# Ten of sixteen MLP blocks form their second product with seven block multiplications

## The chip, the cores and the metric

The kernel runs on one core of a Trainium2 chip. The metric is the device time of one execution in microseconds, as the median of several runs. TensorE multiplies matrices: a weight tile of 128 by 128 is loaded (PEld in the profile), then a moving operand of up to 512 columns streams past it (PE), and the product lands in one of eight PSUM banks. VectorE (DVE) and ScalarE (ACT) work on 128 partitions by some number of elements; SyncE (SP) issues all loads. Each engine runs its own instructions in order and waits on semaphores for the others.

## What is computed

The reference is two layers of a diffusion backbone on T = 1152 tokens (1024 latent, 128 context) of width 1024. Each layer has a token mixer (a Fourier mixer in layer 0, a gated recurrence called HGRN2 in layer 1), and then an MLP with a squared ReLU and a gate:

```
h = rmsnorm(x, norm_mlp[i]) * (1.0 + sc_f) + sh_f
x = x + gt_f * (jnp.square(jax.nn.relu(h @ mlp_w1[i])) @ mlp_w2[i])
```

`mlp_w1` is 1024 by 4096 and `mlp_w2` is 4096 by 1024. The six shift, scale and gate vectors of a layer come from a conditioning matrix `ada_w`.

## The kernel before, in words

Everything is float32. To keep that precision, each operand is split into a high part (`h`, rounded to the format that TensorE reads fast) and a low part (`l`, the rest). `split` does it with a ScalarE copy and a VectorE subtraction, and `mm3` makes three matmuls for each product: high by high, high by low, low by high.

The activations lie transposed, channels on partitions and tokens along the free axis, in three chunks of `CH` = 384 tokens. The MLP of a layer goes through `NBLK` = 8 blocks of four hidden tiles (`FB` = 4, 512 hidden channels). In a block the first product (`up`) takes four hidden tiles by three chunks, eight matmul triples each: 288 matmuls of 384 columns into banks of tag `z`. ScalarE makes ReLU and square, `split` makes the tiles `a0`, `a1`, `a2`. The second product (`out`) takes eight output tiles `d` by three chunks, four triples each: again 288 matmuls of 384 columns, into banks of tag `o`, and VectorE adds each result, times the gate, to the residual `x` in place (`residual`, L594). The weights of the first product come by `unit` (a load of 512 KB into `raw`, then `split`), those of the second by `w2` (256 KB into `raw2`).

Between these, VectorE makes the conditioning vectors (`ada_dve`, L181: two passes of 1024 elements for each of eight loads of a part). Layer 1 needs six such parts, one in each of the blocks 0 to 5 of layer 0, as the code is written. The pool `w` holds the w1 tiles and outlives the MLP; the pool `mlp0` or `mlp1` holds the rest of a block's tiles. A scheduler orders each engine's instructions by priority and readiness, so an instruction may stand well ahead of its place in the code, as far as its buffers allow. A pool that is opened where another was released gets its memory, and its tiles wait for the last use of what lay there.

Of the kernel before, what the change touches and what calls it, by code (L numbers as in the profile page):

```python
# [19 lines left out]
P = 128  # L20
D = 1024
KT = D // P
LS = 1024
LP = 128
T = LS + LP
CH = 384
NC = T // CH
GRID_W = 64
ROWS = LS // GRID_W
NF = 4 * D // P  # L30
FB = 4
NBLK = NF // FB
# [4 lines left out]
PASSES = ((0, 0), (0, 1), (1, 0))  # L37


def spans(c):  # L40

    a, b = c * CH, (c + 1) * CH
    out = []
# [7 lines left out]
def run_all(gen):  # L51
    for _ in gen:
        pass


class Net:
# [132 lines left out]
    def fnet(self):  # L189
# [281 lines left out]
        for d in range(KT):  # L471
# [24 lines left out]
            for xy, a, b, start, step, sc, op in (  # L496
# [40 lines left out]
    def rstd(self, chunks):  # L537

        nc = self.nc
        n = CH // P  # L540
        ps = self.t(self.ps, [P, 512], F32, "m", 2)
# [5 lines left out]
        N = n * len(chunks)  # L547
        r = self.t(self.tp, [P, n * NC], F32, "nrs", 2)[:, 0:N]
        nc.vector.tensor_scalar(out=r, in0=ps[:, 0:N], scalar1=1.0 / D, scalar2=EPS, op0=ALU.mult, op1=ALU.add)
# [45 lines left out]
                                                in1=xs, op0=ALU.mult, op1=ALU.add)  # L595


    def mlp(self, layer, before_chunk, before_block, after_chunk):
        nc, io = self.nc, self.io
        wp = self.pool(f"mlp{layer}")  # L600
        gt = self.mod.get((layer, 5))
# [56 lines left out]
        wp.release()  # L658


    def hgrn(self, xd, after_chunk):
# [312 lines left out]
    def run(self, stop=None):  # L974
        nc, io, tc = self.nc, self.io, self.tc
        self.setup()
        self.fnet()
        self.h = [None] * NC
        self.wp = self.pool("w")
        hp = self.hp = self.pool("hT")  # L980
        rbs = self.rms([0], "o") + self.rms([1, 2], "o")

        ap = self.pool("ada", side="right")

        def ada(blk):
# [3 lines left out]
            if blk < 6:  # L989
                run_all(self.ada_dve(1, blk, ap, ap, 2))  # L990
                if blk == 1:
                    self.make_A(1, 1, 1)
                if blk == 4:
                    self.make_A(1, 4, 3)
            if blk == NBLK - 1:
                ap.release()
                self.cond.release()

        self.mlp(0, lambda c: self.norm_h(c, rbs[c], self.A[0, 4], self.mod[0, 3]), ada, lambda c: self.norm_h(c, *self.rms([c], "m"), self.A[1, 1], self.mod[1, 0]))
# [43 lines left out]
        self.mlp(1, lambda c: None, lambda b: None, final)  # L1043
        dp.release()
        self.ps.release()
        hp.release()
        self.wp.release()
        self.tp.release()
        self.xp.release()
        self.cp.release()  # L1050
# [142 lines left out]
```

## Time and profile before

| | |
|---|---|
| median of 3 runs | 2661.19 us (2660.1 to 2661.51) |
| the profiled execution | 2665.3 us, of which the span in the profile 2663.5 us |
| TensorE busy | 2598.4 us, 98% |
| weight loads busy | 2505.6 us, 94% |
| VectorE busy | 1363.4 us, 51% |
| ScalarE busy | 882.0 us, 33% |
| mean granted TensorE clock | 0.989 |

The profiled execution is 4.1 us above the median of the runs; differences are worked out against it and taken off the median. Busy times of TensorE overlap, since matmuls are pipelined: a matmul's row lasts longer than the distance to the next one's start.

### The profile page before, as it was taken

Reading aid. Unit: us, or ns where it says so; the run is one execution under the profiler, and the core shown is the slowest. Engines: PE = TensorE matmul, PEld = TensorE weight load, DVE = VectorE, ACT = ScalarE, POOL = GpSimd, SP = SyncE. Lnnn points to the kernel's source line nnn. Section 1 sums busy time; section 2 is a strip of 40 time slices with the busy share of each in tenths; the row PEclk is TensorE's granted clock in tenths of the full one; section 3 lists DMA queues with packets and bytes.
Section 4 is the critical chain, followed back from the end, with each engine's and each line's share of the span. In section 5 each row is a group of like instructions: output and inputs, shape, how many; then the busy total and the mean of one; then the engine's idle time right before and its main releaser. Section 6 shows DMA issues by size and latency. Waiting matters only on the chain.

```text
span 2663.5 us, 45518 instructions
## 1 busy us (share of the span) xinstructions
PE 2598.4 (98%) x19446; PEld 2505.6 (94%) x19446; DVE 1363.4 (51%) x2437; ACT 882.0 (33%) x1757; POOL 35.8 (1%) x44
## 2 busy tenths in 40 slices
PE   6999999999999999999999999999999999999999
PEld 3788999999999999999989999899999999999998
DVE  7678998323323338465464664757323323323335
ACT  5435132132132244333432343424331231231232
POOL 0000000000000000000000000000000000000000
PEclk8899999999999999999999999999999999999999
DMA  7543565111111212111011011140111111111111
GB/s 258 185 164 102 172 188 149 47 44 38 47 44 39 58 36 88 33 37 37 29 36 40 31 29 35 37 136 17 56 40 40 48 40 40 48 40 40 48 32 72
DMA packets 65666, 180.00 MB, mean 68 GB/s; under 512 B 8204, under 2 KB 14860, under 8 KB 65464
## 3 DMA queue, kind: packets, MB, share of 16 engines
q1 hardware_dynamic: 65464, 177.09, 21.1%
q8 instruction: 153, 2.51, 0.4%
q14 instruction: 49, 0.40, 0.0%
HBM read 166.57 MB, written 10.49 MB: 66 GB/s over the span
## 4 chain that ended last, share of the span: by engine, by line
PE 87%; DVE 6%; DMA 3%; ACT 2%; issue 2%; POOL 1%; SPq 0%; DVEq 0%; POOLq 0%; ACTq 0%
PE z L91 45%; PE o L91 30%; PE z L729 4%; DMA adaw<-in_ada 2%; DVE junk L181 1%; DVE QK L822 1%; PE m L846 1%; PE o L770 1%; PE o L781 1%; PE m L839 1%; DVE hl L580 1%; PE o L159 0%; PE o L881 0%; ACT sT L785 0%; DVE tmp L577 0%
## 5 line engine op out<-in xcount | busy, mean ns | idle before, releaser
L91 PE MATMUL z<-hh,wh 128*128 128x384 f32 x2496 | 841.4, 338 | 3.9 <-issue 2.0
L91 PE MATMUL z<-hl,wh 128*128 128x384 f32 x2496 | 840.6, 337 | 0.0
L91 PE MATMUL z<-hh,wl 128*128 128x384 f32 x2496 | 838.4, 337 | 0.0
L91 PEld LDWEIGHTS z<-hh,wh 128*128 128x128 f32 x2496 | 468.7, 188 | 10.5 <-issue 3.0
L91 PEld LDWEIGHTS z<-hl,wh 128*128 128x128 f32 x2496 | 469.0, 188 | 3.9 <-DVE hl L580 1.4
L91 PEld LDWEIGHTS z<-hh,wl 128*128 128x128 f32 x2496 | 469.0, 188 | 1.0 <-DVE wl L82 0.2
L594 DVE SCALAR_TENSOR_TENSOR x<-o,mod,x 128x384 f32<-128x384 f32 (+2 forms) x512 | 253.1, 515 | 351.3 <-PE o L91 350.7
L82 DVE TENSOR_TENSOR wl<-raw,wh 128x1024 fp32r<-128x1024 f32 x113 | 138.2, 1223 | 294.4 <-ACT wh L81 294.4
L632 ACT CAST w<-raw 128x512 fp32r<-128x512 f32 x128 | 79.6, 622 | 617.1 <-PE o L91 600.7
L91 PE MATMUL o<-a1h,w 128*128 128x384 f32 x1024 | 280.4, 335 | 0.5 <-DVE x L594 0.5
L91 PE MATMUL o<-a0h,w 128*128 128x384 f32 x1024 | 279.8, 335 | 0.0
L91 PE MATMUL o<-a2h,w 128*128 128x384 f32 x1024 | 278.9, 334 | 0.0
L81 ACT CAST wh<-raw 128x1024 fp32r<-128x1024 f32 x113 | 118.6, 1051 | 271.5 <-PE z L91 229.5
L91 PEld LDWEIGHTS o<-a1h,w 128*128 128x128 f32 x1024 | 186.8, 188 | 1.3 <-DVE x L594 0.8
L91 PEld LDWEIGHTS o<-a0h,w 128*128 128x128 f32 x1024 | 187.4, 189 | 0.5 <-ACT a0h L81 0.2
L609 ACT ACTIVATE s<-z 128x384 f32<-128x384 f32 x192 | 93.6, 489 | 283.0 <-PE z L91 280.8
L91 PEld LDWEIGHTS o<-a2h,w 128*128 128x128 f32 x1024 | 186.6, 188 | 0.6 <-PE o L91 0.3
L91 PE MATMUL o<-a2l,w 128*128 128x384 f32 x512 | 171.9, 336 | 3.6 <-DVE a2l L82 3.6
L822 DVE TENSOR_TENSOR QK<-QK,F 128x1152 f32<-128x1152 f32 x112 | 164.7, 1504 | 17.3 <-ACT nacc L805 13.1
L91 PE MATMUL o<-a0l,w 128*128 128x384 f32 x512 | 171.8, 336 | 0.1
L91 PE MATMUL o<-a1l,w 128*128 128x384 f32 x512 | 171.2, 334 | 0.1
L181 DVE SCALAR_TENSOR_TENSOR junk<-adaw,s_rows 128x1024 bf16<-128x1024 f32 x112 | 136.7, 1220 | 16.7 <-DMA adaw<-in_ada 15.3
(256 smaller groups left out, 3038.0 us busy)
## 6 DMA issues: line engine op xcount, KB each, us to landing
adaw<-in_ada SPq DMA_DIRECT2D x96, 512.0 KB, 4.0
raw<-in_w SPq DMA_DIRECT2D x64, 512.0 KB, 3.6
raw<-in_w SPq DMA_DIRECT2D x128, 256.0 KB, 2.6
raw<-in_win SPq DMA_DIRECT2D x32, 512.0 KB, 3.5
x<-in_xT SPq DMA_DIRECT2D x8, 576.0 KB, 5.5
xd<-x SPq DMA_DIRECT2D x8, 576.0 KB, 2.9
raw<-in_who SPq DMA_DIRECT2D x9, 512.0 KB, 3.6
x<-xd SPq DMA_DIRECT2D x8, 576.0 KB, 5.8
```

Of the source, the lines that this page charges most:

```text
L81: nc.scalar.copy(out=hi, in_=src)
L82: nc.vector.tensor_sub(out=lo, in0=src, in1=hi.bitcast(F32))
L91: self.nc.tensor.matmul(out=out, lhsT=w[a], rhs=h[b], start=first and i == 0, stop=last and i == n - 1)
L181: nc.vector.scalar_tensor_tensor(out=jk, in0=w, scalar=1.0, in1=self.sb[:, b, :], op0=ALU.mult, op1=ALU.mult, accum_out=m[:, j, b:b + 1])
L580: ins = nc.vector.scalar_tensor_tensor(out=lo[:, d, l], in0=t[:, l], scalar=sh[:, d, q:q + 1], in1=hi[:, d, l].bitcast(F32), op0=ALU.add, ...
L594: self.nc.vector.scalar_tensor_tensor(out=xs, in0=ps[:, a - c * CH:b - c * CH], scalar=gt[:, d, q:q + 1], in1=xs, op0=ALU.mult, op1=ALU.add)
L609: nc.scalar.activation(out=s, in_=z, func=AF.Relu)
L632: nc.scalar.copy(out=w[:, 0], in_=raw)
L729: nc.tensor.matmul(out=half, lhsT=hs[c][a][:, KT // 2 * hf + k, o:o + P], rhs=ws[hf][b][:, k, :], start=hf == 0 and k == 0 and m == 0, sto ...
L770: nc.tensor.matmul(out=ps[32 * b:32 * b + 32, c, :], lhsT=lhs(c, b), rhs=rhs(c, b), start=True, stop=True)
L781: nc.tensor.matmul(out=ps[b * W:(b + 1) * W, i, :], lhsT=lhs(cs[0] + i, b), rhs=rhs(cs[0] + i, b ^ 1), start=True, stop=True)
L822: nc.vector.tensor_tensor(out=kv, in0=kv, in1=fv, op=ALU.mult)
```

## The change

In the blocks 3 to 6 of layer 0 and 1 to 6 of layer 1 the second product is done by the new function `mlp_seven`. It divides a block's product into 2 by 2 pieces three ways: the hidden tiles into even and odd (j), the outputs into the tiles d and d + 4 (l), and each half n of the tokens into two quarters (i) of `TQ` = 288. Sums and differences of the four activation pieces and of the four weight pieces are formed first (seven of each), then seven products (p = 0 to 6) replace eight, and they gather in three kinds of bank: `z` takes products 0, 2, 4 and 6, `o` product 1, `m` products 3 and 5. A bank that gathers is read out after each of its products and then added to further: each reading goes into another piece of `x`.

So a block's second product is 4 output pairs d by 7 products by 2 halves n by 2 hidden tiles by 3 passes = 336 matmuls of 288 columns, for 288 of 384 before. The first product keeps its matmuls; its weights come in two halves. ScalarE and VectorE have new work (`put`, the weight sums, 56 read-outs of 288 for 24 of 384). For the first pair, d = 0, the fourteen steps go half by half (all p for n = 0 first). The six conditioning parts of layer 1 are written into blocks 0 to 2 (one, three, two), since the memory of their pool is wanted from block 3 on. The pools `mlp` and `w` are released where the seven-product blocks begin and opened anew where they end; the pool `hT` is now opened ahead of `w`.

```
-    def mlp(self, layer, before_chunk, before_block, after_chunk):
+    def mlp(self, layer, before_chunk, before_block, after_chunk, seven):
...
         for blk in range(NBLK):
+            if blk == seven.start:
+                wp.release()
+                self.wp.release()
+                st = self.pool(f"seven{layer}")
+            if blk in seven:
+                self.mlp_seven(st, layer, blk)
+                before_block(blk)
+                continue
+            if blk == seven.stop:
+                st.release()
+                self.wp = self.pool("w")
+                wp = self.pool(f"mlp{layer}_")
...
+    def mlp_seven(self, st, layer, blk):
...
+            def put(p, n, src):
+
+                hi, lo = ah[k, n][:, p], al[k, n][:, p]
+                nc.scalar.copy(out=hi, in_=src)
+                nc.vector.tensor_sub(out=lo, in0=src, in1=hi.bitcast(F32))
...
+                for h in range(2):
+                    raw = self.t(st, [P, KT // 2, P], F32, "raw", 2)
+                    nc.sync.dma_start(out=raw, in_=io["w1"][layer, blk * FB + 2 * k + j][:, KT // 2 * h:KT // 2 * (h + 1)])
+                    w.append(self.split(st, raw, [P, KT // 2, P], "w", 3))
...
+                        nc.scalar.activation(out=q, in_=q, func=AF.Square)
+                        if j == 0 and i == 0:
+                            put(0, n, q)
+                        elif j == 0:
+                            s3 = self.tmp(TQ)
+                            nc.vector.tensor_sub(out=s3, in0=A[n, 0, 0], in1=q)
+                            put(4, n, s3)
+                        elif i == 0:
+                            put(1, n, q)
+                        else:
+                            put(6, n, q)
+                            a, b, s1 = A[n, 0, 0], A[n, 0, 1], A[n, 1, 0]
+                            nc.vector.tensor_add(out=s1, in0=s1, in1=q)
+                            nc.vector.tensor_sub(out=a, in0=s1, in1=a)
+                            put(2, n, a)
+                            put(3, n, s1)
+                            nc.vector.tensor_sub(out=b, in0=b, in1=a)
+                            put(5, n, b)
...
+            tt = self.t(st, [P, 3, FB // 2, P], F32, "tt", 1)
+            nc.vector.tensor_sub(out=tt[:, 0], in0=B[0, 1], in1=B[0, 0])
+            nc.vector.tensor_sub(out=tt[:, 1], in0=B[1, 1], in1=tt[:, 0])
+            nc.vector.tensor_sub(out=tt[:, 2], in0=B[1, 0], in1=tt[:, 1])
+            wa = self.split(st, raw[0], [P, FB // 2, 2, P], "wa", 1)
+            wb = self.split(st, tt[:, 0:2], [P, 2, FB // 2, P], "wb", 1)
+            nc.vector.tensor_sub(out=B[0, 1], in0=B[1, 1], in1=B[0, 1])
+            wc = self.split(st, raw[1], [P, FB // 2, 2, P], "wc", 1)
+            wd = self.split(st, tt[:, 2], [P, FB // 2, P], "wd", 1)
...
+            plan = (("z", 0, 0), ("o", 0, 0), ("z", 0, 1), ("m", 1, 1), ("z", 1, 1), ("m", 0, 1), ("z", 1, 0))
...
+            steps = [(p, n) for p in range(7) for n in range(2)]
+            if d == 0:
+                steps.sort(key=lambda s: s[1])
...
+                for k in range(FB // 2):
+                    for m, (x, y) in enumerate(PASSES):
+                        nc.tensor.matmul(out=ps, lhsT=W[p][k][x], rhs=(ah, al)[y][k, n][:, p, :],
...
+                        xs = self.x[d + KT // 2 * l][:, a:b]
+                        nc.vector.scalar_tensor_tensor(out=xs, in0=ps[:, a - t0:b - t0],
+                                                       scalar=gt[:, d + KT // 2 * l, q:q + 1], in1=xs,
+                                                       op0=ALU.mult, op1=ALU.add)
...
+        hp = self.hp = self.pool("hT")
         self.wp = self.pool("w")
-        hp = self.hp = self.pool("hT")
...
+            for part in ((0,), (1, 2, 3), (4, 5))[blk] if blk < 3 else ():
+                run_all(self.ada_dve(1, part, ap, ap, 2))
```

Three places of the order of instructions. The first is VectorE where the second product of a block of layer 1 begins. Before, the low parts of the last activation tiles (`a2l`) and the residuals of the first output tile alternate, with one waiting for each:

```order
L82 TENSOR_TENSOR a2l_23318<-s_23314,a2h_23317 128x384 [waits Activation_49]
L82 TENSOR_TENSOR a0l_23356<-s_23352,a0h_23355 128x384 [waits Activation_49]
L82 TENSOR_TENSOR a1l_23388<-s_23384,a1h_23387 128x384 [waits Activation_49]
L82 TENSOR_TENSOR wl_23912<-raw_23909,wh_23911 128x1024 [waits DVE_49,DMAHW6_49,PE_49,Activation_49]
L594 SCALAR_TENSOR_TENSOR x_2447_17257<-o_23428,mod_5_6993,x_2447_17257 128x384 [waits PE_49]
L82 TENSOR_TENSOR a2l_23420<-s_23416,a2h_23419 128x384 [waits Activation_49]
L594 SCALAR_TENSOR_TENSOR x_2447_17257<-o_23442,mod_5_6993,x_2447_17257 128x384 [waits PE_49]
```

In the changed kernel (a block in the middle of layer 1; L779 reads out a bank, L691 is `put`'s subtraction, L730 to L734 are sums) the same place reads:

```order
L83 TENSOR_TENSOR wl_23091<-raw_23088,wh_23090 128x512 [waits DMAHW7_49,PE_49,Activation_49]
L779 SCALAR_TENSOR_TENSOR x_2551_18141<-z_22471,mod_5_4613,x_2551_18141 128x288 [waits PE_49]
L730 TENSOR_TENSOR nacc_22209<-nacc_22209,tmp_22432 128x288 [waits Activation_49]
L691 TENSOR_TENSOR al_22208<-tmp_22401,ah_22207 128x288 [waits Activation_49]
L691 TENSOR_TENSOR al_22208<-tmp_22432,ah_22207 128x288 [waits Activation_49]
L731 TENSOR_TENSOR nacc_22209<-nacc_22209 128x288 [waits DVE_49]
L691 TENSOR_TENSOR al_22208<-nacc_22209,ah_22207 128x288 [waits Activation_49]
L734 TENSOR_TENSOR tmp_22401<-tmp_22401,nacc_22209 128x288 [waits DVE_49]
L691 TENSOR_TENSOR al_22208<-nacc_22209,ah_22207 128x288 [waits Activation_49]
L779 SCALAR_TENSOR_TENSOR x_2551_18141<-o_22479,mod_5_4613,x_2551_18141 128x288 [waits PE_49]
L691 TENSOR_TENSOR al_22208<-tmp_22401,ah_22207 128x288 [waits Activation_49]
L779 SCALAR_TENSOR_TENSOR x_2565_18285<-z_22471,mod_5_4613,x_2565_18285 128x288 [waits PE_49]
```

Between the first two readings of bank `z_22471` now stand ten instructions, eight of them for the second half's activations. TensorE has its third product for this bank, `z_22471<-ah_21964,wch_22463 [waits DVE_49]`, 43 matmuls behind the first of the second product.

The second place is SyncE ahead of the last block of layer 1 (the name in_w stands for both weights; L588 is the w1 load, L630 the w2 load). Before, the w1 loads of the last block stand ahead of the last four w2 loads of the block before it:

```order
L630 DMA raw_3257_23567<-in_w 128x512 [waits DMAHW4_49,DMAHW2_49,DVE_49]
L588 DMA raw_23807<-in_w 128x1024 [waits DVE_49]
L588 DMA raw_23909<-in_w 128x1024 [waits DVE_49]
L588 DMA raw_24011<-in_w 128x1024 [waits DMAHW5_49,DVE_49]
L588 DMA raw_24113<-in_w 128x1024 [waits DMAHW6_49,DVE_49]
L630 DMA raw_3262_23615<-in_w 128x512 [waits DMAHW3_49,DVE_49]
```

Now (L741 is the w2 load of `mlp_seven`, L589 the w1 load of the last block):

```order
L741 DMA raw_3525_25872<-in_w 128x512 [waits DMAHW5_49,DVE_49]
L741 DMA raw_3526_25874<-in_w 128x512 [waits DMAHW6_49,DVE_49]
L589 DMA raw_26011<-in_w 128x1024 [waits PE_49]
L589 DMA raw_26113<-in_w 128x1024 [waits PE_49]
L643 DMA raw_3603_26423<-in_w 128x512 [waits DMAHW3_49]
```

They moved behind all loads of the block before, and wait for TensorE: the first for the seventh product of the last pair d in its first half, six matmuls ahead of that block's end, the second for the last matmul.

The third place is VectorE at the start of the first MLP, where the norm's factors (L561) become the first chunk (L577, L580). Before:

```order
L561 TENSOR_TENSOR tmp_392_2112<-ident_58,nrs_391_2109 128x384
L561 TENSOR_TENSOR tmp_396_2126<-ident_58,nrs_395_2123 128x384
L561 TENSOR_TENSOR tmp_398_2130<-ident_58,nrs_395_2123 128x384
L577 SCALAR_TENSOR_TENSOR tmp_408_2154<-x0_289_1277,A0_4_2068,o_393_2114 128x384
L577 SCALAR_TENSOR_TENSOR tmp_409_2158<-x1_290_1280,A0_4_2068,o_393_2114 128x384
```

Now:

```order
L562 TENSOR_TENSOR tmp_398_2130<-ident_58,nrs_395_2123 128x384
L83 TENSOR_TENSOR wl_402_2143<-raw_400_2140,wh_401_2142 128x1024
L578 SCALAR_TENSOR_TENSOR tmp_408_2154<-x0_289_1277,A0_4_2068,o_393_2114 128x384
L83 TENSOR_TENSOR wl_405_2149<-raw_403_2146,wh_404_2148 128x1024
L581 SCALAR_TENSOR_TENSOR hl0_407_2153<-tmp_408_2154,mod0_3_1598,hh0_406_2152 128x384
```

The low parts of the first two w1 tiles, which stood among the Fourier mixer's last instructions, moved into the norm's chain.

## Rows read from the trace of the kernel before

**Rows 1.** The page: span, and busy time of the engines.
```profile
span 2663.5 us, 45518 instructions
PE 2598.4 (98%) x19446; PEld 2505.6 (94%) x19446; DVE 1363.4 (51%) x2437; ACT 882.0 (33%) x1757; POOL 35.8 (1%) x44
```

**Rows 2.** Windows (stretch, length, busy time and instructions of each engine, clock, DMA).
```profile
204.00:310.00 106.00, 101.44 (x528) 94.39 (x529) 94.00 (x185) 41.38 (x83) 2.43 (x2) 0.94 0.41 128
...
1949.00:1999.00 50.00, 50.00 (x290) 50.00 (x290) 11.16 (x17) 20.34 (x37) 0.00 (x0) 1.00 0.13 38
1999.00:2049.00 50.00, 50.00 (x290) 50.00 (x289) 20.93 (x39) 6.83 (x11) 0.00 (x0) 1.00 0.16 48
```

**Rows 3.** The chain that ended last (start, length, what, matmuls).
```profile
1069.83 26.00 PE z L729 x216
...
1949.49 49.92 PE z L91 x288
1999.41 49.92 PE o L91 x288
```

**Rows 4.** TensorE's timeline in the Fourier mixer (start, length, matmul).
```profile
137.43 0.28 PE L91 MATMUL o<-EY1h,vh 128*128 128x256 f32 x1
...
138.68 0.28 PE L91 MATMUL o<-EY1h,vl 128*128 128x256 f32 x1
...
197.20 0.31 PE L91 MATMUL o<-EX1h,vh 128*128 128x322 f32 x1
...
198.83 0.31 PE L91 MATMUL o<-EX1h,vl 128*128 128x322 f32 x1
```

**Rows 5.** Groups by line and shape (busy us, mean ns, idle before).
```profile
L594 DVE SCALAR_TENSOR_TENSOR x<-o,mod,x 128x384 f32<-128x384 f32 x256 | 157.8, 617 | 207.6 <-PE o L91 207.6
L82 DVE TENSOR_TENSOR wl<-raw,wh 128x1024 fp32r<-128x1024 f32 x113 | 138.2, 1223 | 294.4 <-ACT wh L81 294.4
...
L81 ACT CAST wh<-raw 128x1024 fp32r<-128x1024 f32 x113 | 118.6, 1051 | 271.5 <-PE z L91 229.5 <-DMA raw<-in_who 18.4 <-PE z L729 15.7
L610 ACT ACTIVATE s<-s 128x384 f32<-128x384 f32 x192 | 100.9, 527 | 5.9
...
L633 DVE TENSOR_TENSOR w<-raw,w 128x512 fp32r<-128x512 f32 x128 | 87.7, 686 | 7.8 <-ACT w L632 7.6
...
L729 PEld LDWEIGHTS z<-wh,hl 128*128 128x128 f32 x288 | 55.3, 192 | 0.0
...
L594 DVE SCALAR_TENSOR_TENSOR x<-o,mod,x 128x128 f32<-128x128 f32 x128 | 43.7, 342 | 0.0
...
L82 DVE TENSOR_TENSOR a1l<-s,a1h 128x384 fp32r<-128x384 f32 x64 | 35.7, 557 | 182.8 <-ACT a1h L81 182.8
...
L81 ACT CAST a1h<-s 128x384 fp32r<-128x384 f32 x64 | 32.9, 514 | 1.9
```

**Rows 6.** VectorE's timeline, three instructions in a row, one span.
```profile
1000.41 1.67 DVE L577 SCALAR_TENSOR_TENSOR tmp<-x,A,m 128x384 f32<-128x384 f32 x3 [0.54 <-PE m L564]
```

**Rows 7.** Loads of w1: queue, count, size, median us from issue to landing.
```profile
raw<-in_w SPq DMA_DIRECT2D x64, 512.0 KB, 3.6
```

**Rows 8.** Windows of 2 us in the Fourier mixer and behind it.
```profile
132.00:134.00 2.00, 2.00 (x11) 2.00 (x11) 1.30 (x2) 0.23 (x1) 0.00 (x0) 0.50 0.75 296
134.00:136.00 2.00, 2.00 (x10) 2.00 (x10) 0.97 (x3) 0.52 (x2) 0.00 (x0) 0.50 0.69 175
136.00:138.00 2.00, 2.00 (x15) 2.00 (x13) 1.01 (x1) 0.37 (x1) 0.00 (x0) 0.84 0.98 392
...
202.00:204.00 2.00, 0.09 (x1) 0.00 (x0) 1.56 (x5) 1.38 (x4) 0.00 (x0) 1.00 0.49 94
...
206.00:208.00 2.00, 1.69 (x8) 1.60 (x8) 0.27 (x2) 0.00 (x0) 0.30 (x2) 0.50 0.85 321
```

**Rows 9.** VectorE's timeline at the start of the first MLP.
```profile
209.57 1.03 DVE L561 TENSOR_TENSOR tmp<-ident,nrs 128x384 f32<-128x384 f32 x2 [1.21 <-POOL nrs L550]
...
213.74 1.67 DVE L580 SCALAR_TENSOR_TENSOR hl<-tmp,mod,hh 128x384 fp32r<-128x384 f32 x3
```

More of the change, by code (lines that the diff above doesn't have):

```diff
@@ L26 @@
 CH = 384
+TQ = T // 4
 NC = T // CH
@@ L595, in residual @@
                                                 in1=xs, op0=ALU.mult, op1=ALU.add)
-    def mlp(self, layer, before_chunk, before_block, after_chunk):
+    def mlp(self, layer, before_chunk, before_block, after_chunk, seven):
         nc, io = self.nc, self.io
         wp = self.pool(f"mlp{layer}")
-        gt = self.mod.get((layer, 5))
         for blk in range(NBLK):
+            if blk == seven.start:
[10 more added lines that the diff above has]
+                wp = self.pool(f"mlp{layer}_")
             a = {}
@@ L658, in mlp @@
         wp.release()
+    def mlp_seven(self, st, layer, blk):
+        nc, io = self.nc, self.io
+        gt = self.mod[layer, 5]
+        ah, al = {}, {}
+        for k in range(FB // 2):
+            for n in range(2):
+                ah[k, n], al[k, n] = (self.t(st, [P, 7, TQ], F32R, "a" + s, FB) for s in "hl")
+            def put(p, n, src):
+                hi, lo = ah[k, n][:, p], al[k, n][:, p]
+                nc.scalar.copy(out=hi, in_=src)
+                nc.vector.tensor_sub(out=lo, in0=src, in1=hi.bitcast(F32))
+            one = self.t(self.tp, [P, T], F32, "nacc", 1)
+            A = {(g // 2, g % 2, 0): one[:, g * TQ:(g + 1) * TQ] for g in range(4)}
+            for j in range(2):
+                w = []
+                for h in range(2):
+                    raw = self.t(st, [P, KT // 2, P], F32, "raw", 2)
+                    nc.sync.dma_start(out=raw, in_=io["w1"][layer, blk * FB + 2 * k + j][:, KT // 2 * h:KT // 2 * (h + 1)])
+                    w.append(self.split(st, raw, [P, KT // 2, P], "w", 3))
+                for c in range(NC):
+                    z = self.t(self.ps, [P, 512], F32, "z", 3)[:, 0:CH]
+                    self.mm3(z, [([q[:, m % (KT // 2), :] for q in w[m // (KT // 2)]], [q[:, m, :] for q in self.h[c]])
+                                 for m in range(KT)])
+                    for g in range(4):
+                        lo, hi = max(g * TQ, c * CH), min((g + 1) * TQ, (c + 1) * CH)
+                        if lo >= hi:
+                            continue
+                        n, i = g // 2, g % 2
+                        if (n, i, j) not in A:
+                            A[n, i, j] = self.tmp(TQ)
+                        q = A[n, i, j]
+                        nc.scalar.activation(out=q[:, lo - g * TQ:hi - g * TQ], in_=z[:, lo - c * CH:hi - c * CH],
+                                             func=AF.Relu)
+                        if hi < (g + 1) * TQ:
+                            continue
+                        nc.scalar.activation(out=q, in_=q, func=AF.Square)
[16 more added lines that the diff above has]
+                            put(5, n, b)
+        for d in range(KT // 2):
+            raw = []
+            for l in range(2):
+                raw.append(self.t(st, [P, FB // 2, 2, P], F32, "raw2", 2))
+                nc.sync.dma_start(out=raw[l], in_=io["w2"][layer, blk, d + KT // 2 * l].rearrange("p (k j) c -> p k j c", j=2))
+            B = {(j, l): raw[l][:, :, j, :] for j in range(2) for l in range(2)}
+            tt = self.t(st, [P, 3, FB // 2, P], F32, "tt", 1)
[7 more added lines that the diff above has]
+            wd = self.split(st, tt[:, 2], [P, FB // 2, P], "wd", 1)
+            W = [[[q[:, k, 0] for q in wa] for k in range(2)], [[q[:, k, 1] for q in wa] for k in range(2)],
+                 [[q[:, 1, k] for q in wb] for k in range(2)], [[q[:, 0, k] for q in wb] for k in range(2)],
+                 [[q[:, k, 0] for q in wc] for k in range(2)], [[q[:, k, 1] for q in wc] for k in range(2)],
+                 [[q[:, k] for q in wd] for k in range(2)]]
+            acc = {}
+            plan = (("z", 0, 0), ("o", 0, 0), ("z", 0, 1), ("m", 1, 1), ("z", 1, 1), ("m", 0, 1), ("z", 1, 0))
+            LAST = {(t, max(p for p in range(7) if plan[p][0] == t)) for t in "zom"}
+            steps = [(p, n) for p in range(7) for n in range(2)]
+            if d == 0:
+                steps.sort(key=lambda s: s[1])
+            for p, n in steps:
+                tag, i, l = plan[p]
+                first = (tag, n) not in acc
+                if first:
+                    acc[tag, n] = self.bank(tag)[:, 0:TQ]
+                ps = acc[tag, n]
+                for k in range(FB // 2):
+                    for m, (x, y) in enumerate(PASSES):
+                        nc.tensor.matmul(out=ps, lhsT=W[p][k][x], rhs=(ah, al)[y][k, n][:, p, :],
+                                         start=first and k == 0 and m == 0,
+                                         stop=(tag, p) in LAST and k == FB // 2 - 1 and m == 2,
+                                         skip_group_check=True)
+                t0 = (2 * n + i) * TQ
+                for a, b, q in ((t0, min(t0 + TQ, LS), 0), (max(t0, LS), t0 + TQ, 1)):
+                    if a < b:
+                        xs = self.x[d + KT // 2 * l][:, a:b]
+                        nc.vector.scalar_tensor_tensor(out=xs, in0=ps[:, a - t0:b - t0],
+                                                       scalar=gt[:, d + KT // 2 * l, q:q + 1], in1=xs,
+                                                       op0=ALU.mult, op1=ALU.add)
@@ L988, in ada @@
                     run_all(self.ada_dve(0, 5, ap, ap, 2))
[L989 to L995, printed above, removed]
+            for part in ((0,), (1, 2, 3), (4, 5))[blk] if blk < 3 else ():
+                run_all(self.ada_dve(1, part, ap, ap, 2))
+            if blk == 2:
+                self.make_A(1, 1, 1)
+                self.make_A(1, 4, 3)
                 ap.release()
                 self.cond.release()
-        self.mlp(0, lambda c: self.norm_h(c, rbs[c], self.A[0, 4], self.mod[0, 3]), ada, lambda c: self.norm_h(c, *self.rms([c], "m"), self.A[1, 1], self.mod[1, 0]))
+        self.mlp(0, lambda c: self.norm_h(c, rbs[c], self.A[0, 4], self.mod[0, 3]), ada, lambda c: self.norm_h(c, *self.rms([c], "m"), self.A[1, 1], self.mod[1, 0]), range(3, NBLK - 1))
         dp = self.pool("spill", space=DRAM)
@@ L1041, in final @@
                     nc.sync.dma_start(out=io["y"][i][:, h * 512:(h + 1) * 512], in_=o)
-        self.mlp(1, lambda c: None, lambda b: None, final)
+        self.mlp(1, lambda c: None, lambda b: None, final, range(1, NBLK - 1))
         dp.release()
         self.ps.release()
+        self.wp.release()
         hp.release()
-        self.wp.release()
         self.tp.release()
```

## The prediction

> **What bounds the kernel now.** I read the page first. TensorE is busy for 98% of the span and its weight loads for 94%, VectorE for half [rows 1]. The reader is to see that no other engine is near; where it is idle it waits for TensorE. The windows show it for the stages that the change touches: in the 50 us of an MLP's first product VectorE works 11.2 us and ScalarE 20.3, in the 50 us of the second 20.9 and 6.8, and TensorE has the full clock in both [rows 2]. Then the chain of waits: each of the two products is one piece of 288 matmuls in 49.92 us without a stop [rows 3], so one matmul of 384 columns takes 49.92 / 288 = 173.3 ns. A change to the second product is therefore paid in full, as long as the other engines keep up.
>
> **The gain: 336 matmuls of 288 columns for 288 of 384.** No row has 288 columns. The product of 256 columns in the chain gives 26.00 / 216 = 120.4 ns [rows 3]; a line through it and 173.3 gives 120.4 + 32 x 0.413 = 133.6 ns. A third size lies near that line: 322 columns, eleven steps in 1.63 us, 148.2 ns (line: 147.7) [rows 4]. Below, the Fourier mixer's 256 columns go at 1.25 / 11 = 113.6 ns [rows 4], and the same 6.9 ns beyond 256 / 2.4 would give 126.9 for 288. Above, the 256-column rate by the column (0.470 ns) would give 135.4. I take 133.5, since three of the four rows agree on it: 336 x 0.1335 = 44.86 us, 5.06 less than 49.92. Ten blocks: **-50.6** (bounds -73 and -44).
>
> **At the head of the second product: a stall.** Before, the low parts and residuals alternate there and TensorE doesn't stop [rows 3]. Now the order on VectorE (the second listing of the first place above) puts eight sums and subtractions of the second half between the first two readings of a `z` bank. ScalarE's work after the last matmul of the first product is a cast of a half weight tile, two ReLUs and two squares. Casts of 384 and 1024 take 514 and 1051 ns and a square of 384 527 [rows 5], so by a line 0.84 ns a column: 0.62 + 0.29 + 3 x 0.45, with handing over some 2.4 us. VectorE follows with about ten instructions of 288 columns: a subtraction takes 557 ns for 384 and 686 for 512 [rows 5], so about 0.46, a reading 0.51 (between 342 for 128 and 617 for 384). With one round trip to ScalarE for `put(2)` (0.45 and handing over) the reading of the second `z` product ends at 2.4 + 4.7 + 0.5, less a little overlap: 7.1 to 7.4 us. TensorE comes to the third `z` product after 42 x 0.1335 = 5.6 us plus two short waits of 0.25, since with the first pair ordered half by half only one step of 0.8 us lies between a `z` product and the next. It waits 0.8 to 1.0 more. I take 1.4 a block (bounds 0.5, the short waits alone, and 3.5, if the chain goes by full durations with a handing over at each step): **+14** for ten.
>
> **Behind the head: hidden.** For a pair d VectorE has 12 readings of 288, two split at the latent's end into 160 and 128 columns, three subtractions of 512 and five sums of 256 (about 0.42): 6.2 + 1.4 + 2.1 + 2.1 = 11.8 us by full durations. Three instructions in a row take 1.67 us, not 3 x 0.617 [rows 6], so each overlaps the next by 0.09; 24 instructions make 9.6. TensorE needs 84 x 0.1335 = 11.2 for a pair. A bank comes again four steps later, so its reading has three steps, 2.4 us, of slack. I cost it at nothing; without that cover it is the third rival. The first product also gets work: ScalarE about 32 of 49.9 us and VectorE 25, by the counts in the code and the same durations. I take nothing for that either.
>
> **Where the run of seven-product blocks begins** (block 3 of layer 0, block 1 of layer 1) the pools are released, and the low part of the first half tile stands behind the last readings of the block before on VectorE: some handing over, a cast 0.62 and a subtraction 0.69, where the third matmul is due 0.35 us (2 x 173 ns) after the last. I estimate 1.2 each: **+2.4** (0 to 4).
>
> **Where it ends** (block 7 of each layer) the listing of the second place shows the w1 loads waiting for TensorE: the first may start when the seventh product's first half is done, six matmuls (0.8 us) ahead of the end. Then come 3.6 us until it has landed [rows 7], a cast of 1.05 and a subtraction of 1.22 [rows 5], and some 0.5 for four handings over. The third matmul comes at 6.4 - 0.8 = 5.6 us instead of 0.35: 5.25 each, **+10.5** (4 to 6 each; the first and second matmul fit inside). SyncE itself has nothing else behind these loads but w2 loads that are due 50 us later.
>
> The clock may fall in those gaps. In the Fourier mixer, behind a stretch with few matmuls, the granted clock is 0.50 from 132 on and up to about 136.6 (0.84 in 136 to 138), with TensorE busy throughout [rows 8]; half of 4.5 us is lost. At the first MLP the window 202 to 204 has TensorE busy 0.09 us at the full clock, and 206 to 208 is at half [rows 8]. So a gap of 5 us may lead to the lower level: I take 2.0 each, **+4** (bounds 0 and 4.5).
>
> **The first MLP's start.** Two `wl` of 1.22 us [rows 5] moved into the norm's chain (the third place above). There VectorE goes from 209.57 to the readings at 213.74 with hardly a gap [rows 9], and TensorE waits for its result; the whole window 204 to 310 has VectorE at 94 of 106 us [rows 2]. Two at 1.1 (with overlap): **+2.2** (0 to 2.5).
>
> **The conditioning** in blocks 0 to 2: 94 of 106 us says that already before, the first block carries it as fast as VectorE can, and the order of these instructions is nearly that of before. Nothing (0 to 1). The shifted pools put no other load behind a new wait that I found: nothing.
>
> **Sum:** -50.6 + 14 + 2.4 + 10.5 + 4 + 2.2 = -17.5. The profiled execution took 2665.3 us; 2647.8 after. The median of the runs lies 4.1 below it, so I forecast **2644 us**.
>
> **Rivals.**
>
> A, the sum above, 0.60. Its own range goes from 2622 (pace 131, head 0.5, clock 0) to 2656 (pace 135.4, head 2).
>
> B, the stalls come out small and the pace is the Fourier mixer's, 126.9 ns: -73 + 10 + 18 of the rest = -45, **2616 us**. For it: the 113.6 ns are the same kind of matmul at the same clock. Against it: two long runs say 120.4 and 173.3. 0.13.
>
> E, the head eats the gain: 3.5 us a block, with every step of VectorE's chain waiting for ScalarE or for its own last result. -50.6 + 35 + 19 = +3, **2664 us**. For it: the ten instructions do depend on each other, so the overlap of [rows 6] may be missing there. Against it: the copies that they need are ScalarE's only work by then. 0.11.
>
> C, slower: VectorE becomes the bound of the second product. The point is 12.5 us a pair (49.92 / 4): above it, the new product is longer than the old. By full durations a pair has 11.8, four of them 47.1, and with 5 us of the head's chain 52.1: 2.2 more than before in each block, +22, and the other terms +19: **2702 us**. For it: readings that wait for TensorE each time lose the overlap, and a reading of a bank may be slower than the mean of 617. Against it: 617 is already a reading of a bank, and mostly behind a wait [rows 5]. 0.13.
>
> D, slower: the load of weights sets the pace, not the columns. Every matmul has its own load, so 336 of them at 173.3 ns take 58.2 us, +8.3 a block: 83 + 19, **2763 us**. Against it: the loads of the 256-column product take 192 ns as well [rows 5], and it runs at 120.4 ns a matmul, so they overlap. 0.03. The Trainium skill ("Perfetto Trace Analysis", Identifying the Most-Contended Engine) says that busy matmuls tell little of how full TensorE is and that the busy share of the weight loads should be looked at; by that share, 94%, the load side is nearly full and more loads should cost. The trace speaks against such a reading: loads of 192 ns every 120.4 ns.
>
> The Trainium skill ("TensorE: Matmul & The Clock Gate", Back-to-back issue gap) also gives a single matmul's gap as N / 2.4 + 2.5 ns; for 384 and 288 columns that is 162.5 and 122.5, an estimate of 46.8 to 41.2 us for the product and -56 for ten blocks in place of -50.6. The trace has 173.3 for 384 [rows 3], so I keep the rows.
>
> **Range and chances.** C and D hold 0.16 and lie above every other case; a range that ends between E and C and starts within B leaves out them and about a third of B: **2612 to 2668**. A measurement of this kernel can tell some 0.2% from no change, 5.3 us. Faster (below 2655.9): A but for 0.03, and B, and a little of E, **0.71**. Same: the 0.03 of A and 0.07 of E, **0.10**. Slower: C, D and the rest of E, **0.19**.
>
> **What would show it.** In the changed kernel's chain, second products of about 44.9 us plus a stop; in TensorE's timeline behind the head, steps of 133.5 ns. At the head, one wait of about 1 us for a reading (L779) and two short ones. At the two ends of the runs, 5 us of TensorE idle, first for the load of `raw`, then for `wl`, and the clock at half behind it if I am right on that. At the first MLP, two `wl` between L562 and L581. In windows of the second product, VectorE near 40 of 45 us and never the one waited for, except at the head. The prediction is wrong if VectorE is waited for in every pair, if the steps are nearer 127 or 145 ns, or if a load or a pool holds TensorE at the start of every block, which I found no sign of.

## The result and the profile after

The changed kernel takes 2631.82 us (median of 4 runs, 2628.45 to 2634.58), the kernel before beside it 2660.64 (2659.82 to 2661.51): ratio 0.9891, 95% interval 0.9877 to 0.9905, so 28.8 us less. The profiled execution took 2631.1 us. The one of before, on which the prediction's sum stands, took 2665.3; between these two it is 34.2 us, and the stages below are read from them.

The page after, span and busy time (the same rows of before are [rows 1]):

```profile
span 2629.3 us, 48079 instructions
...
PE 2555.0 (97%) x19926; PEld 2456.1 (93%) x19926; DVE 1690.3 (64%) x3397; ACT 974.9 (37%) x2197; POOL 35.6 (1%) x44
```

The chain that ended last, after (start, length, what, matmuls; that of before is [rows 3]). The lines with `z L92` and some 288 matmuls are first products:

```profile
478.62 49.93 PE o L92 x288
529.98 49.35 PE z L92 x283
...
718.73 49.94 PE z L92 x288
...
813.38 49.94 PE z L92 x288
...
906.93 3.53 DMA raw<-in_w
912.89 51.26 PE z L92 x285
964.16 22.90 PE o L92 x132
...
1888.86 49.93 PE o L92 x288
1940.21 49.33 PE z L92 x283
...
2105.03 3.19 PE z L771 x24
...
2412.93 49.94 PE z L92 x288
...
2506.46 3.50 DMA raw<-in_w
2511.14 53.12 PE z L92 x288
```

The reader is to see three things. From the end of a first product (718.73 + 49.94 = 768.67) to the start of the next (813.38) it is 44.7 us where it was 49.92. The steps inside are 3.19 / 24 = 133 ns. And the first product of block 7 begins late, behind a load of 3.5 us, in both layers, and is longer than 49.9.

In numbers, after less before:
- the second product, ten times 44.7 less 49.92: -52;
- the first product where the runs of seven-product blocks begin (from 528.55 to 579.33, and 1938.79 to 1989.54): 50.8 each, +1.7 together;
- the first product of block 7: with 44.7 us for the product before it, from 908.0 to 964.16 and from 2507.6 to 2564.26, 56.1 and 56.7 us, +13.0 together;
- up to the end of the first product of block 2 in layer 0, which is the start of the second product behind it: 478.62 after, 474.97 before (the line below), +3.65;
- the recurrence and the last stage: -0.7.

The sum is -34.3, the 34.2 that were measured.

```profile
474.97 49.92 PE o L91 x288
```

The stretch from this point to the end of the span tells more than the whole span: it takes 2188.5 us before (474.97 to 2663.5) and 2150.7 after (478.62 to 2629.3), 37.8 less. What lies ahead of it differs by some us between two executions of the same kernel. Against the 28.8 of the medians it leaves a cost of some 9 us ahead of this point.

### The profile page after: what moved, and what is told of

Its sections match the earlier page's. It is cut to its first block, busy times and chain, and to the rows that moved or that the text cites. A ratio compares the mean times of both kernels' runs of the same rounds, so it can differ in the third digit from the quotient of the medians.

```text
span 2629.3 us, 48079 instructions
## 1 busy us (share of the span) xinstructions
PE 2555.0 (97%) x19926; PEld 2456.1 (93%) x19926; DVE 1690.3 (64%) x3397; ACT 974.9 (37%) x2197; POOL 35.6 (1%) x44
## 4 chain that ended last, share of the span: by engine, by line
PE 87%; DVE 6%; DMA 3%; ACT 2%; issue 2%; POOL 1%; SPq 0%; DVEq 0%; POOLq 0%; ACTq 0%
PE z L92 46%; PE o L92 12%; PE z L771 10%; PE m L771 5%; PE z L852 4%; PE o L771 2%; DMA adaw<-in_ada 2%; PE m L969 1%; DVE junk L182 1%; PE o L893 1%; DVE QK L945 1%; PE o L904 1%; PE m L962 1%; DVE hl L581 1%; DVE wl L83 1%
## 5 line engine op out<-in xcount | busy, mean ns | idle before, releaser
L92 PE MATMUL z<-hh,wh 128*128 128x384 f32 x2496 | 842.6, 339 | 9.8 <-ACT wh L82 7.7
L92 PE MATMUL z<-hl,wh 128*128 128x384 f32 x2496 | 842.6, 338 | 0.7 <-DVE hl L581 0.5
L92 PE MATMUL z<-hh,wl 128*128 128x384 f32 x2496 | 840.0, 337 | 1.6 <-DVE wl L83 1.6
L92 PEld LDWEIGHTS z<-hh,wh 128*128 128x128 f32 x2496 | 469.5, 188 | 17.4 <-ACT wh L82 8.7
L92 PEld LDWEIGHTS z<-hl,wh 128*128 128x128 f32 x2496 | 470.2, 188 | 6.1 <-DVE hl L581 3.6
L92 PEld LDWEIGHTS z<-hh,wl 128*128 128x128 f32 x2496 | 470.0, 188 | 4.0 <-DVE wl L83 3.2
L83 DVE TENSOR_TENSOR wl<-raw,wh 128x512 fp32r<-128x512 f32 (+1 forms) x153 | 144.3, 944 | 209.1 <-ACT wh L82 208.9
L82 ACT CAST wh<-raw 128x512 fp32r<-128x512 f32 (+1 forms) x153 | 126.3, 826 | 255.1 <-PE z L92 157.7
L779 DVE SCALAR_TENSOR_TENSOR x<-z,mod,x 128x288 f32<-128x288 f32 (+2 forms) x400 | 171.9, 452 | 14.7 <-PE z L771 13.0
L595 DVE SCALAR_TENSOR_TENSOR x<-o,mod,x 128x384 f32<-128x384 f32 (+1 forms) x192 | 95.1, 514 | 75.6 <-PE o L92 74.9
L691 DVE TENSOR_TENSOR al<-tmp,ah 128x288 fp32r<-128x288 f32 x160 | 71.2, 455 | 65.7 <-ACT ah L690 61.4
L92 PE MATMUL o<-a0h,w 128*128 128x384 f32 x384 | 105.2, 340 | 1.1 <-DVE x L595 1.1
L92 PE MATMUL o<-a1h,w 128*128 128x384 f32 x384 | 105.3, 337 | 0.0
L92 PE MATMUL o<-a2h,w 128*128 128x384 f32 x384 | 103.8, 335 | 0.0
L779 DVE SCALAR_TENSOR_TENSOR x<-m,mod,x 128x288 f32<-128x288 f32 (+2 forms) x200 | 87.2, 453 | 9.9 <-PE m L771 9.4
L852 PE MATMUL z<-wh,hh 128*128 128x256 f32 x288 | 81.8, 284 | 0.0
L852 PE MATMUL z<-wh,hl 128*128 128x256 f32 x288 | 81.7, 284 | 0.0
```

What stands on the lines that cost most here:

```text
L82: nc.scalar.copy(out=hi, in_=src)
L83: nc.vector.tensor_sub(out=lo, in0=src, in1=hi.bitcast(F32))
L92: self.nc.tensor.matmul(out=out, lhsT=w[a], rhs=h[b], start=first and i == 0, stop=last and i == n - 1)
L595: self.nc.vector.scalar_tensor_tensor(out=xs, in0=ps[:, a - c * CH:b - c * CH], scalar=gt[:, d, q:q + 1], in1=xs, op0=ALU.mult, op1=ALU.add)
L691: nc.vector.tensor_sub(out=lo, in0=src, in1=hi.bitcast(F32))
L779: nc.vector.scalar_tensor_tensor(out=xs, in0=ps[:, a - t0:b - t0], scalar=gt[:, d + KT // 2 * l, q:q + 1], in1=xs, op0=ALU.mult, op1=ALU.add)
```

## The head of a second product

ScalarE's last two squares in the changed kernel and VectorE's timeline from there to the reading of the second `z` product; then TensorE's timeline at the product's first matmul and at the third product for this bank (`wch`):

```profile
2085.00 0.78 ACT L718 ACTIVATE tmp<-tmp 128x288 f32<-128x288 f32 x2
```

```profile
2085.30 0.51 DVE L779 SCALAR_TENSOR_TENSOR x<-z,mod,x 128x288 f32<-128x288 f32 x1
2085.80 0.46 DVE L730 TENSOR_TENSOR nacc<-nacc,tmp 128x288 f32<-128x288 f32 x1
2086.18 0.82 DVE L691 TENSOR_TENSOR al<-tmp,ah 128x288 fp32r<-128x288 f32 x2
2086.92 0.45 DVE L731 TENSOR_TENSOR nacc<-nacc 128x288 f32<-128x288 f32 x1
...
2088.39 0.51 DVE L779 SCALAR_TENSOR_TENSOR x<-o,mod,x 128x288 f32<-128x288 f32 x1
2088.82 0.45 DVE L691 TENSOR_TENSOR al<-tmp,ah 128x288 fp32r<-128x288 f32 x1
2089.19 0.51 DVE L779 SCALAR_TENSOR_TENSOR x<-z,mod,x 128x288 f32<-128x288 f32 x1
```

```profile
2084.01 0.29 PE L771 MATMUL z<-ah,wah 128*128 128x288 f32 x1
...
2089.67 0.35 PE L771 MATMUL z<-ah,wah 128*128 128x288 f32 x1
2089.86 0.30 PE L771 MATMUL z<-ah,wch 128*128 128x288 f32 x1
```

The ten instructions are those that were listed, in that order: nine between the two readings (the listing's text says ten), and the second reading itself. But they start every 0.37 to 0.38 us (from 2085.80 to 2089.19 nine steps), and none waits for ScalarE, which is done with its squares at 2085.78. The reading ends at 2089.70, 5.7 us after the product's first matmul, not 7.1 to 7.4, and TensorE comes to the third product for this bank at 5.8. That product's first matmul starts 0.19 us after the one ahead of it, where a step is 0.13: TensorE loses less than 0.1 us there.

## The end of a run

Windows around the start of the last block of layer 1 in the changed kernel (stretch, length, busy time and instructions of PE, PEld, DVE, ACT, POOL, then clock, DMA share, GB/s), and ScalarE's and VectorE's timeline there:

```profile
2508.00:2510.00 2.00, 0.00 (x0) 0.00 (x0) 0.30 (x2) 0.00 (x0) 0.00 (x0) 1.00 0.78 303
2510.00:2512.00 2.00, 0.86 (x3) 0.82 (x3) 0.88 (x1) 1.04 (x1) 0.00 (x0) 0.59 0.93 327
2512.00:2514.00 2.00, 2.00 (x7) 1.61 (x6) 0.89 (x2) 1.63 (x3) 0.00 (x0) 0.50 0.54 179
2514.00:2516.00 2.00, 2.00 (x8) 2.00 (x7) 1.88 (x3) 0.46 (x1) 0.00 (x0) 0.50 0.67 231
2516.00:2520.00 4.00, 4.00 (x21) 4.00 (x21) 0.00 (x0) 1.19 (x3) 0.00 (x0) 0.85 0.69 248
```

```profile
2510.04 1.04 ACT L82 CAST wh<-raw 128x1024 fp32r<-128x1024 f32 x1 [13.19 <-DMA raw<-in_w]
...
2511.12 1.22 DVE L83 TENSOR_TENSOR wl<-raw,wh 128x1024 fp32r<-128x1024 f32 x1 [2.82 <-ACT wh L82]
```

It is the forecast's order of events: the load, the cast at 2510.04, the subtraction at 2511.12 that ends at 2512.34, 4.7 us after the product's end at 2507.6 (the forecast had 5.6). TensorE, which had no matmul from 2507.6 to 2511.14, then goes at half the clock (the lower level, 1.2 of 2.4 GHz) from 2512 to 2516, busy throughout, and gets the full clock within the next window.

## Experiments

In all of them the changed kernel is the start; shown is what differs from it.

**The changed kernel again** (after_again). 

> The changed kernel itself, as the measure for the runs beside it. If its gain is a matter of stages (product 44.7 us for 49.9, ten times, less 13 us at the two ends of the runs), it lies 27 to 32 us below the kernel before again, and its spread tells what difference the others can show. If the load times of the first MLP decide, it may lie several us off.

Measured: 2633.37 us (2632.15 to 2633.9), ratio 0.9887 (0.9874 to 0.9901). From the end of block 2's first product on it takes 2150.7 us again (481.44 to 2632.1); that end itself lies at 481.44 for 478.62. So some 3 us between two executions come from the stages before, and smaller differences than that are not told by a single run. That stretch, and the chain block by block, tell some 0.2 us.

**Without the order by halves** (unsorted):

```
-            if d == 0:
-                steps.sort(key=lambda s: s[1])
```

> The first pair is no longer ordered half by half. Theory 1, the head's chain on VectorE ends in time either way (the second half's activations are ready 3.7 us after the product's start, and in the plain order they are wanted after 4.0 us): same as the changed kernel within 3 us. Theory 2, the order by halves is what hides the chain, as my forecast supposed with a head that is late by 1.4 us: the plain order costs 1 us or more a block, 10 us or more in all.

Measured: 2631.15 us (2630.74 to 2634.88), the same, and 2150.9 us from block 2's first product on. Theory 1 holds: the plain order costs nothing.

**Four more sums at the head** (head_plus4). The added sums change the second half's activations.

```
                             put(6, n, q)
+                            if n == 1 and k == 1:
+                                for _ in range(4):
+                                    nc.vector.tensor_add(out=A[n, 0, 0], in0=A[n, 0, 0], in1=q)
```

> Four more sums of 288 columns stand in VectorE's chain at the head of each second product (they change the second half's activations). Theory 1, the chain ends just when TensorE comes to the third product of bank z, with no slack: four times 0.37 to 0.45 us are paid, 1.5 us a block, 15 us in all. Theory 2, the head has slack of its own and nothing is waited for: 0 to 3 us in all.

Measured: 2636.68 us (2630.21 to 2641.86), unclear by itself. The chain is clear:

```profile
2138.07 49.94 PE z L92 x288
2233.35 49.94 PE z L92 x288
```

A block takes 95.28 us for 94.65 (718.73 to 813.38), so 0.6 of the 1.5 us are paid; the stretch from block 2's first product on is 8.1 us longer. Neither theory: VectorE's timeline shows why.

```profile
2193.03 0.45 DVE L734 TENSOR_TENSOR nacc<-nacc 128x288 f32<-128x288 f32 x1
2193.40 0.51 DVE L782 SCALAR_TENSOR_TENSOR x<-z,mod,x 128x288 f32<-128x288 f32 x1
2193.83 0.45 DVE L737 TENSOR_TENSOR tmp<-tmp,nacc 128x288 f32<-128x288 f32 x1
```

The reading of the second `z` product (L782) now stands ahead of a sum and two subtractions that it stood behind. It needs nothing of them: it reads the first half. The scheduler moved it. TensorE stops later instead, by 0.34 us at one place, where the profile names ScalarE's cast of the next pair's weight sums (`wbh`); the changed kernel has no such wait. That the longer chain is what delays this cast is argued, not shown.

**Activation tiles behind the weight tiles** (w_first). A pool's memory is dealt out in the order in which its tiles are first asked for.

```
         for k in range(FB // 2):
-            for n in range(2):
-                ah[k, n], al[k, n] = (self.t(st, [P, 7, TQ], F32R, "a" + s, FB) for s in "hl")
...
                     w.append(self.split(st, raw, [P, KT // 2, P], "w", 3))
+                if j == 0:
+                    for n in range(2):
+                        ah[k, n], al[k, n] = (self.t(st, [P, 7, TQ], F32R, "a" + s, FB) for s in "hl")
```

> The activation tiles of a seven-product block are allocated behind the weight tiles, so that the first w1 load of block 7 takes memory that is free long before and waits for no matmul. Theory 1, the two gaps (6.2 and 7.0 us before block 7) are the load, the cast and the subtraction one after another, with the clock behind: the load and cast are hidden, and 9 to 12 us are gained over the changed kernel. Theory 2, the gap is rather the last readings on VectorE and the release of the pool, or the load is held elsewhere in its queue: 0 to 4 us are gained.

Measured: 2619.79 us (2616.52 to 2624.99), ratio 0.9844 (0.983 to 0.9857): 13.6 us less than the changed kernel beside it, and the fastest version. The chain, and TensorE's waits from block 1 of layer 1 up to its last block (total, times, longest):

```profile
2403.35 49.94 PE z L92 x288
2499.93 49.69 PE z L92 x285
```

```profile
PE z L92 <- DVE wl L83: 1.9, 2, 1.3
```

From 2498.0 (2403.35 + 49.94 + 44.7) the last first product ends at 2549.62, 51.6 us later for 56.7. What is left is one subtraction behind the last readings on VectorE. By the chain the two ends give back 9.6 us (4.5 and 5.1), and the stretch from block 2's first product on is 9.3 shorter; the rest of the 13.6 lies ahead of that (this product ends at 473.3 here) and is of the size of what separates two executions. Theory 1 holds. TensorE still stops for 1.3 us, and the clock stays at 1.00 behind it:

```profile
2500.00:2502.00 2.00, 2.00 (x12) 2.00 (x13) 1.64 (x3) 1.23 (x2) 0.00 (x0) 1.00 0.88 224
```

**Three blocks fewer** (fewer3): layer 1's run is `range(4, NBLK - 1)`. 

> In layer 1 the seven products are done in blocks 4 to 6 alone, in three blocks fewer. Theory 1, each such block is worth 5.2 us (44.7 for 49.92, with next to no stop at its head): 15.6 us above the changed kernel. Theory 2, a block is worth what my sum had, 5.06 less 1.4 for the stop: 11 us above it.

Measured: 2645.32 us (2641.05 to 2646.86), 13.5 above the changed kernel's median, and 18.1 below the kernel before beside it where the changed kernel lay 28.8 below. That is 13.5 or 10.7, and the medians don't tell the theories apart. Its chain does:

```profile
472.93 49.93 PE o L92 x288
```

From there to the end of its span (2639.3) it is 2166.4 us, 15.7 more than the changed kernel's 2150.7: Theory 1, 5.2 a block.

**Only the last reading of a bank** (last_reading). Left out are 32 of the 56 readings of a block.

```
                 t0 = (2 * n + i) * TQ
+                if (tag, p) not in LAST:
+                    continue
```

> Left out: the readings of a bank after all but its last product, 32 of 56 in a block. VectorE has some 14 us less to do in a second product. Theory 1, VectorE is hidden and a step of 132.5 ns is set by its 288 columns: within 3 us of the changed kernel. Theory 2, VectorE's readings of the banks slow the matmuls: steps nearer 127 ns, 1.8 us a block, 15 to 18 us less.

Measured: 2626.16 us (2624.67 to 2629.97). Blocks in its chain, and the window of one second product:

```profile
2128.89 49.94 PE z L92 x288
2223.38 49.94 PE z L92 x288
```

```profile
2084.20:2128.80 44.60, 44.60 (x338) 44.60 (x337) 28.18 (x63) 12.19 (x25) 0.00 (x0) 1.00 0.19 54
```

VectorE's busy time falls from 42.4 to 28.2 us, and a block takes 94.5 us for 94.65. The pace is that of the matmuls. Theory 1 holds for the blocks. The median is 5.7 us lower, where 3 were allowed: 1.5 lie in the ten blocks, and the stretch from block 2's first product on is 1.8 us shorter in all, so the others lie ahead of it, where two executions differ by some 3 us anyway.

**The readings of m twice** (m_twice). Each is repeated into an unused tile.

```
+                        if tag == "m":
+                            scr = self.t(self.tp, [P, T], F32, "nacc", 1)
+                            nc.vector.tensor_scalar(out=scr[:, 0:b - a], in0=ps[:, a - t0:b - t0],
+                                                    scalar1=gt[:, d + KT // 2 * l, q:q + 1], scalar2=None, op0=ALU.mult)
```

> Each reading of an m bank is done a second time into a tile that nobody uses, four readings of 288 more for a pair (one split in two). VectorE is busy for 42.3 of 44.7 us in a second product. Theory 1, it is hidden by that margin alone: 4 x 4 x 0.43 to 0.5 make 7 to 8 us more, 2.4 of them fit, and 4.5 to 6 us a block are paid, 45 to 60 in all, so that the gain is gone. Theory 2, much of the busy time is overlap or waiting and there is room: under 10 us in all.

Measured: 2651.16 us (2649.54 to 2652.64), ratio 0.9955 (0.994 to 0.997), some 19 us above the changed kernel's median. One second product of the changed kernel, and then one of this kernel, in windows (the second starts 0.85 us ahead of its product); then VectorE's timeline here, and TensorE's waits in the same stretch:

```profile
2084.00:2128.90 44.90, 44.90 (x339) 44.81 (x338) 42.35 (x102) 12.05 (x25) 0.00 (x0) 1.00 0.19 54
```

```profile
2092.90:2140.30 47.40, 46.26 (x341) 45.45 (x340) 45.88 (x115) 10.29 (x23) 0.00 (x0) 1.00 0.16 46
```

```profile
2111.07 0.51 DVE L779 SCALAR_TENSOR_TENSOR x<-m,mod,x 128x288 f32<-128x288 f32 x1
2111.50 0.51 DVE L784 TENSOR_SCALAR nacc<-m,mod 128x288 f32<-128x288 f32 x1
```

```profile
PE z L771 <- DVE wal L83: 1.0, 1, 1.0
```

Added are 20 readings a block, 12 of 288 at 0.43 us from start to start, 4 of 160 and 4 of 128 at about 0.3 and 0.25: 7.4 us. The first products of layer 1 start every 96.7 us (2043.81, 2140.52) for 94.65, so 2.0 to 2.1 are paid and 5.3 fit. By the busy row only some 2.5 us were free. Of the 2.0, 1.0 is the wait for `wal` in the row above; the others are shorter stops. Neither theory had the size: VectorE is waited for now, but later than its busy time says.

**No seven-product block** (no_seven, no_seven_again): the range is `range(NBLK, NBLK)` in both layers, so only the other edits are left. 

> No block is done with seven products; the other edits stay (conditioning in blocks 0 to 2, pool hT ahead of w). Theory 1, these edits cost what the trace shows at the first MLP (two low parts of w1 in the norm's chain, and a wait on ScalarE, 2.2 to 3.7 us): 2 to 4 us above the kernel before. Theory 2, the start differs between two runs by chance of the loads and the edits cost nothing: within 2 us of the kernel before.

 And the second time: 

> The kernel with no seven-product block once more, as the measure for the next one: 4 to 8 us above the kernel before, as in its first run.

Measured: 2668.91 us (ratio 1.0026, 1.0016 to 1.0036) and 2668.57 (1.0028, 1.0018 to 1.0038), 5.5 and 7.9 us above the medians of the kernel before beside them. Theory 1 has the sign, and the cost is larger than it had.

**The conditioning alone** (cond_only): as no_seven, with the pools as before.

```
+        self.wp = self.pool("w")
         hp = self.hp = self.pool("hT")
-        self.wp = self.pool("w")
```

> No seven-product block, and the pool w lies below hT again as in the kernel before, so that the low parts of the first two w1 tiles stand among the Fourier mixer's instructions; of the change only the conditioning in blocks 0 to 2 is left. Theory 1, the two low parts in the norm's chain are paid: 2 to 3 us less than with no seven-product block, and 2 to 5 us above the kernel before are left to the conditioning. Theory 2, the conditioning's new places alone cost it: as slow as with no seven-product block.

Measured: 2663.87 us, ratio 1.0008 (0.9998 to 1.0017): not to be told from the kernel before, and 4.7 us below no_seven_again beside it. So the order of the pools costs some 5 us, and the conditioning's places 0 to 4 by the interval. TensorE's waits from the norm ahead of the first MLP to block 2 differ mainly in these rows, first with the new order of the pools (no_seven_again), then with the old:

```profile
PE o L92 <- DVE a2l L83: 4.6, 2, 2.6
PE z L92 <- ACT hh L580: 0.9, 3, 0.5
PE z L92 <- DVE hl L581: 0.9, 3, 0.4
```

```profile
PE o L92 <- DVE a2l L83: 3.8, 2, 2.2
PE z L92 <- ACT hh L580: 0.5, 1, 0.5
```

The waits for `hl` are new, and those for `hh` longer: the two low parts of w1 stand ahead of the pieces of the norm. These rows hold about 2.1 us of the 5; where the rest goes is open.

**Block 0 of layer 1 as well** (from0): w_first with `range(0, NBLK - 1)` in layer 1. 

> The activation tiles behind the weight tiles as in the kernel that gained by it, and block 0 of layer 1 done with seven products too. That block then takes its chunks of tokens in the order of the hidden tiles, so it wants the last chunk after 8 us instead of after 25. Theory 1, that wait is longer than the 5.2 us that a block is worth and the 1.4 us of the pools' change before block 1: 0 to 15 us above that kernel. Theory 2, the last chunk's norm is ready by then: 5 to 7 us below it.

Measured: 2621.8 us (2619.49 to 2622.28), 2 us above w_first, and 3.5 above it in the stretch from block 2's first product on (2144.9 and 2141.4). TensorE's waits from the last norm of layer 1 into block 0:

```profile
PE z L92 <- DVE wl L83: 2.9, 1, 2.9
PE m L546 <- DVE nacc L536: 2.1, 1, 2.1
PE o L565 <- DVE tmp L562: 1.8, 1, 1.8
```

The last chunk's norm (the rows with `nacc` and `tmp`), which was covered in w_first but for 0.7 us, is waited for, and so is the low part of the block's first weights, 2.9 us for 0.6. Theory 1, near its lower end.

**The conditioning two by two** (w_first_even): w_first with the parts `((0, 1), (2, 3), (4, 5))`. 

> As the kernel with the activation tiles behind the weight tiles, with the conditioning parts two by two in blocks 0 to 2 instead of one, three, two. Theory 1, VectorE is the bound of blocks 0 and 1 wherever the parts stand: within 3 us of that kernel. Theory 2, the three parts of block 1 are its costly place: 3 to 6 us less.

Measured: 2619.56 us (2617.43 to 2621.44), as w_first. Theory 1.

## Why the prediction was right, and where its sizes were off

The mechanism was right: the second product's pace is set by its matmuls, and each of the ten blocks is paid in full. The sizes were not: 28.8 us less were measured, and 17.5 forecast.

The pace: forecast 133.5 ns, measured 132.5 to 133. The line through the rows of 256 and 384 columns [rows 3] was the better guide; the pace by the Fourier mixer's 113.6 ns [rows 4], rival B, did not come. The Trainium skill ("TensorE: Matmul & The Clock Gate", Back-to-back issue gap) gives a single matmul's gap as 122.5 for 288 columns, an estimate by its formula; the trace has 10 more.

**The term that was furthest off is the head's, +14.** About 0.2 us a block were lost in all (44.7 for 336 x 0.1325 = 44.5, an estimate from these rows), 2 us in ten; the wait of about 1 us that the prediction named as a sign did not come. The order of VectorE's instructions was read rightly. But I gave them full durations and a round trip to ScalarE, 4.7 + 0.5 less a little, although [rows 6] were used one paragraph later to take the overlap off. They start every 0.37 us and end 3.9 us after ScalarE's squares; and ScalarE is ready at 1.8 us instead of 2.4. So the chain ends just about when TensorE needs it. head_plus4 adds that the reading's place in that order is no dependence: it is moved when the chain grows.

VectorE behind the head: hidden, as forecast. Rival C is excluded by last_reading, which takes a third off VectorE's busy time and leaves the blocks alone; m_twice shows that VectorE begins to cost time some 5 us of work a block further on. E is excluded by the 44.7 us, and D by the steps of 133 ns.

Into the runs: 1.7 for 2.4. Out of them: 13.0 for 10.5 + 4, with the load, the cast, the subtraction and then the clock in the order named. The low part `wl` came 4.7 to 4.8 us after the product's end, and three matmuls (0.5 us) fit ahead of it: about 4.3 us each of waiting, so some 4.4 of the 13.0 are the clock's, an estimate from these rows. w_first takes the load and the cast out of the gap, 1.3 us of it are left, and the clock does not fall.

The first MLP's start was mis-sized the other way, 2.2 forecast and some 5 measured for the order of the pools, with 0 to 4 for the conditioning (forecast 0 to 1).

Together: from block 2's first product on, 37.8 us less were measured and 19.7 forecast (-50.6 + 14 + 2.4 + 10.5 + 4). Of these 18 us the head is 12, the pace 3.5 and the two ends 2. Ahead of it the cost was some 9 us, of which no_seven shows 5.5 to 7.9, where 2.2 were forecast: 7 us the other way. That the forecast lies only 12 us above the result is in part luck: the two errors have opposite signs.

## What to carry to other kernels

Cost a chain of short instructions by the distance from start to start in a run of them, not by the duration in a group's row; here 0.37 for 0.46, with a round trip to ScalarE that was covered, made most of the difference between a wait of 1 us and none. Where a pool is released and another opened in the middle of a stream, look at which old tiles lie under the first load of the new one: asking for the short-lived tiles first was worth about as much here as two seven-product blocks. A change of places that costs nothing by its code (the order of two pools) can move work into a chain that the bound engine waits for, so it wants a run of its own.

## What the runs showed of the hardware that was not expected

VectorE's busy share overstates how full it is. In the second product it is busy for 42.35 of 44.9 us, 94%, and 7.4 us more work a block cost 2.0 (m_twice). A reading of 288 columns that waits for its operand shows 0.51 us, and one that follows another without a wait starts 0.43 after it, so a stretch of separate readings is counted longer than it would take in one run. The Trainium skill ("Perfetto Trace Analysis", Identifying the Most-Contended Engine) calls the busy share of VectorE a fair measure of how close it is to its limit; m_twice speaks against that for short instructions.

After 3.5 us without a matmul (2507.6 to 2511.14), the granted clock was 0.50 to 0.59 with TensorE working again, up to 2516, and that product took 53.12 us from its first line in the chain for 49.92. The forecast had allowed for this fall, at 2.0 us each. With 1.3 us of the gap left in w_first, the clock stayed at 1.00.
